# Last projection of a hybrid decoder layer: 8 of its 22 feature blocks by seven quarter products in place of eight, with the residual kept in DRAM meanwhile

## The chip, the core and the metric

The kernel runs on one core of a Trainium2 chip. The metric is the time of one execution on the device, in microseconds (us); the kernel before takes 1056.22 us (median of 3 runs, 1055.83 to 1057.02). A core has TensorE (PE; "PEld" is its weight load), VectorE (DVE), ScalarE (ACT), GpSimd (POOL) and SyncE (SP), which here only issues DMA transfers. PE writes to PSUM, 8 banks of 128 x 512 f32; all else lies in SBUF or DRAM.

## What is computed

One layer on 512 tokens of width 1024: a gated mixer of three branches, then a gated feed-forward part, then a norm. The change touches the last product of the feed-forward part:

```python
x = x + merged @ w_o[i]
x = x + conv_ffn(rmsnorm(x, ln2_g[i]), ffn_w_up[i], ffn_conv_w[i], ffn_conv_b[i], ffn_w_down[i])
...
return rmsnorm(x, final_g)

def conv_ffn(u, w_up, conv_w, conv_b, w_down):
    h = causal_dwconv(u @ w_up, conv_w, conv_b)
    a, v = h[..., :D_FF], h[..., D_FF:]
    return (jax.nn.silu(a) * v) @ w_down        # (512 x 2816) @ (2816 x 1024), f32
```

## The kernel before

Every f32 operand is split in two parts that PE takes as f32r: a high part (an ACT copy) and a low part (a DVE subtraction, operand minus high). A product is then three matmuls: high by high, high by low, low by high. `mm3` (lines 215 to 222) issues them in that order, so the low part of the weights is first wanted after two thirds of a group.

The work is a list of **jobs** (`Job`, line 72). A job is one piece of weights, at most 1 MiB, and a body that multiplies with it. While job n runs, `prepare` (lines 1281 to 1292) has queued, in this order: DVE makes the low part of job n+1 (`low`, line 204); ACT makes the high part of job n+2 in two halves (`cast`, line 184); SP fetches the weights of job n+3 (`fetch`, line 174). There are two buffers for raw weights, three for high parts and two for low parts. The order on PE, ACT, DVE and POOL is the order in which the program issues the instructions (`ORDERED`, line 1304); every engine takes its instructions in order, so one that waits holds up all behind it. SP's order is set by the scheduler of the framework.

Small work beside the matmuls stands in generators. `step()` (line 143) advances each by one piece; bodies call it between their tiles. `T()` hands out 54 SBUF tiles of 128 x 512, `MM()` and `SM()` four PSUM banks each.

The stages at the end of the program (`program`, line 1098) are:

- **wo_jobs** (line 936), the product with w_o, 8 jobs; it adds to the residual tiles X1[tb, h] (token block tb of 4, column half h), which lie in 8 of the 54 tiles from there to the end.
- **up_jobs** (line 1022), 22 jobs of 256 columns each, with 48 matmuls of 512 columns. `up_evac` (line 998) takes each tile out of PSUM (ACT line 1000, DVE line 1003 twice), applies silu (line 1005) and multiplies the two halves on POOL (line 1008). `later` (line 1010) then splits the feature block k of 22 into `ACTS[k]`, high fh (ACT line 1016) and low fl (DVE line 1017); the blocks 0 to 3 lie in `wide`.
- **down_jobs** (line 1075), the last projection. For each column half h there are 6 jobs: five of 4 feature blocks (48 matmuls: 4 token blocks x 4 blocks x 3) and one of 2 (24 matmuls). The four token blocks accumulate in four banks over all 22 blocks. For h = 0 the result is added to X1 (line 1078) and the first part of the final norm is done; for h = 1 the last two jobs are held and run token block by token block, each followed by the second part of the norm and the stores to the output.

In all the last projection has 2 x 4 x 22 x 3 = 528 matmuls of 512 columns.

Of the kernel before, what the change touches and what calls it, by code (L numbers as in the profile page):

```python
# [10 lines left out]
F32 = mybir.dt.float32  # L11
F32R = mybir.dt.float32r
# [4 lines left out]
P = 128  # L17
# [11 lines left out]
SH = 16  # L29
DFF = 2816  # L30
KF = DFF // P
C_Q, C_K, C_V = 0, AW, 2 * AW
C_POOL = 3 * AW
C_Z = C_POOL + D
# [37 lines left out]
class Job:  # L72


    def __init__(self, parts, k, c, body):
        self.parts, self.k, self.c, self.body = parts, k, c, body
        self.raw = self.split = None
        self.late = self.short = False


@with_exitstack
def trunk(ctx: ExitStack, tc, out, x, rel_bias, ln1_g, w_in, b_gate, w_a, pool_w, pool_scale, w_b,
# [23 lines left out]
    def T(name, dt=F32, shape=(P, S)):  # L106
        return big.tile(list(shape), dt, name=name, tag="t")

    def MM(name):
        return psum.tile([P, S], F32, name=name, tag="mm")  # L110
# [55 lines left out]


    def fetch(job, cuts=1):
        raw = job.raw = wraw.tile([P, job.k, job.c], F32, name="raw", tag="raw")
        at = 0  # L170
        for src in job.parts:
            n = src.shape[-1] // cuts
            for i in range(cuts):
                sp.dma_start(raw[:, :, at:at + n], src[:, :, i * n:(i + 1) * n])
                at += n

    def cast(job, cuts=1, spread=False):

        w = job.c // cuts
        job.high = whp.tile([P, job.k, job.c], F32R, name="wh", tag="wh")  # L180

        def high(i):
            o = slice(i * w, (i + 1) * w)
            act.copy(job.high[:, :, o], job.raw[:, :, o])  # L184

        def at(i):
            high(i)
            if i + 1 < cuts:
                second.append(lambda: at(i + 1))

        if spread:
            second.append(lambda: at(0))
            return
        for i in range(cuts):
            high(i)
# [16 lines left out]
    def wsrc(w, k0, k1, c0, c1):  # L212
        return w[k0 * P:k1 * P, c0:c1].rearrange("(k p) c -> p k c", p=P)

    def mm3(ps, wh, wl, xh, xl, ks, first=True, last=True, flip=False):

        n, total = 0, 3 * len(ks)
        for a, b in ((wh, xh), (wh, xl), (wl, xh)):
            for k in ks:
                l, r = (b(k), a(k)) if flip else (a(k), b(k))  # L220
                pe.matmul(ps, l, r, start=first and n == 0, stop=last and n == total - 1)  # L221
                n += 1
# [18 lines left out]
            yield Job([wsrc(w, 0, nk, c0 + i * P, c0 + i * P + width)], nk, width, body)  # L241

    def jobs_b(parts_of, c, xh, xl, nk, evac, kstep=4, mk=None, blocks=range(4), tail=0,
               turn_over=False):


        acc = {}
        starts = list(range(0, nk, kstep))
        held = []

        def use(k0, k1, ws, tb):
            wh, wl = ws
            mm3(acc[tb][:, :c], lambda k: wh[:, k - k0, :], lambda k: wl[:, k - k0, :],
                lambda k: xh(k, tb), lambda k: xl(k, tb), range(k0, k1),
                k0 == 0, k1 == nk, flip=True)

        for n, k0 in enumerate(starts):
            k1 = min(nk, k0 + kstep)

            def body(ws, n=n, k0=k0, k1=k1):  # L260
                if n == 0:
                    for tb in blocks:
                        acc[tb] = (mk or MM)("pb")
                late = n >= len(starts) - tail
                if late:
                    held.append((k0, k1, ws))
                if late and n < len(starts) - 1:
                    return
                for tb in blocks:
                    for a in (held if late else [(k0, k1, ws)]):  # L270
                        use(*a, tb)
                    if k1 == nk:
                        evac(tb, acc[tb])
                    if tb % 2:
                        step()
            job = Job(parts_of(k0, k1), k1 - k0, c, body)
            job.short = len(blocks) < 4
            if turn_over and n == len(starts) - 1:
                job.late = True

                def body(ws, job=job, inner=body):
                    late_split.append(job.prepare(later=True))
                    inner(ws)
                job.body = body
            yield job
# [643 lines left out]
    def load_x1():  # L929
        nxt["g2"] = grow(ln2_g[0])  # L930
        for tb in range(4):
            for h in range(2):
                t = X1[tb, h] = T("x1")
                sp.dma_start(t, x[tb * P:(tb + 1) * P, h * S:(h + 1) * S])

    def wo_jobs(pair, h):
        def evac(tb, ps):
            t = X1[tb, h]
            dve.tensor_tensor(t, t, ps, OP.add)
            if h == 0:  # L940
                nxt[tb] = norm_early(t, nxt["g2"])
                return
            if "uh" not in nxt:
                nxt["uh"] = upool.tile([P, KD, S], F32R, name="uh2", tag="uh")
                nxt["ul"] = upool.tile([P, KD, S], F32R, name="ul2", tag="ul")
            v0, xg0 = nxt[tb]
            us = [T("u0"), T("u1")]
            it = norm_late(t, nxt["g2"], v0, lambda xg1: ((us[0], xg0), (us[1], xg1)))
            next(it)

            def rest():
                next(it, None)
# [45 lines left out]
    def up_evac(m, ps):  # L998
        t = HC[m] = T("hc")
        act.activation(t, ps, AF.Identity, bias=ff["c1"][:, ff["b"] + m:ff["b"] + m + 1], scale=fw(2, m))  # L1000
        for k in range(2):
            sh = 2 - k
            dve.scalar_tensor_tensor(t[:, sh:], ps[:, :S - sh], fw(k, m), t[:, sh:], OP.mult, OP.add)  # L1003
        if m < KF:
            act.activation(t, t, AF.Silu)
            return
        a = HC[m - KF]
        pool.tensor_tensor(a, a, t, OP.mult)  # L1008

        def later():  # L1010
            yield
            k = m - KF
            if k == 0:
                wide.extend(ypool.tile([P, 4, S], F32R, name=n, tag="xs") for n in ("fh", "fl"))
            h, l = (t[:, k, :] for t in wide) if k < 4 else (T("fh", F32R), T("fl", F32R))
            act.copy(h, a)
            dve.tensor_sub(l, a, h.bitcast(F32))
            ACTS[k] = (h, l)

        running.append(later())  # L1020

    def up_jobs():
        held = []
# [48 lines left out]

    fin = {}

    def down_jobs(h):
        def evac(tb, ps):
            t = X1[tb, h]
            dve.tensor_tensor(t, t, ps, OP.add)
            if h == 0:
                fin[tb] = norm_early(t, fin["g"])  # L1080
                return
            v0, xg0 = fin[tb]
            for _ in norm_late(t, fin["g"], v0, lambda xg1: ((xg1, xg1), (xg0, xg0))):
                xg1 = _
            for i, o in ((1, xg1), (0, xg0)):
                sp.dma_start(out[tb * P:(tb + 1) * P, i * S:(i + 1) * S], o)

        return jobs_b(lambda k0, k1: [wsrc(w_down, k0, k1, h * S, h * S + S)], S,
                      lambda k, tb: ACTS[k][0][:, tb * P:(tb + 1) * P],
                      lambda k, tb: ACTS[k][1][:, tb * P:(tb + 1) * P], KF, evac,  # L1090
                      mk=(MM, SM)[h], tail=2 if h else 0)


    class Call:
# [3 lines left out]
    def program():  # L1098
# [26 lines left out]
        for pair in range(2):  # L1125
            for h in range(2):
                yield from wo_jobs(pair, h)
            if pair == 0:
                yield Call(ff_cols)
        yield from up_jobs()  # L1130
        yield Call(lambda: fin.setdefault("g", grow(final_g)))
        yield Call(finish)
        yield from down_jobs(0)
        yield from down_jobs(1)

    jobs = list(program())
    weights = [j for j in jobs if isinstance(j, Job)]
# [200 lines left out]
```

## Time and profile before

| | |
|---|---|
| median of 3 runs | 1056.22 us |
| the execution that was profiled | 1058.24 us |
| its span, first to last instruction | 1056.4 us |
| PE busy | 1044.1 us (99% of the span) |
| DVE, ACT, POOL busy | 576.7, 430.9, 134.9 us |
| read from DRAM | 110.87 MB |
| stage of line 221, tile pu (up_jobs), in the chain | 229.33 us, x1056 |
| stage of line 221, tile pb after it (down_jobs), in the chain | 119.69 us, x528 |
| from the last matmul to the end | 7.3 us |

In the views a group of instructions reads: line, engine, operation, result <- operands by tile name, shapes, number (x); then busy us and mean ns of one; then the idle time of the engine before them and what ended it. "wh" and "wl" are the high and low part of weights, "raw" the weights as fetched, "pb" the PSUM tile of the last projection. A view by windows gives the busy time of each engine in each stretch of the span, then the granted clock of PE (PEclk, 1.00 is full), the busy share of the 16 DMA engines, and the GB/s that they moved.

### The profile page before, as it was taken

Reading aid. Unit: us, or ns where it says so; the run is one execution under the profiler, and the core shown is the slowest. Engines: PE = TensorE matmul, PEld = TensorE weight load, DVE = VectorE, ACT = ScalarE, POOL = GpSimd, SP = SyncE. Lnnn points to the kernel's source line nnn. Section 1 sums busy time; section 2 is a strip of 40 time slices with the busy share of each in tenths; the row PEclk is TensorE's granted clock in tenths of the full one; section 3 lists DMA queues with packets and bytes.
Section 4 is the critical chain, followed back from the end, with each engine's and each line's share of the span. In section 5 each row is a group of like instructions: output and inputs, shape, how many; then the busy total and the mean of one; then the engine's idle time right before and its main releaser. Section 6 shows DMA issues by size and latency. Waiting matters only on the chain.

```text
span 1056.4 us, 13018 instructions
## 1 busy us (share of the span) xinstructions
PE 1044.1 (99%) x5268; PEld 872.5 (83%) x5268; DVE 576.7 (55%) x777; ACT 430.9 (41%) x698; POOL 134.9 (13%) x118
## 2 busy tenths in 40 slices
PE   8999999999999999999999999999999999999997
PEld 8878889898788887787888888898888888888885
DVE  5552523245667538576658756766556565532315
ACT  6343412232545633567555323554444434431311
POOL 1580000000000001100143500002111111110100
PEclk9999999999999999999999999999999999999999
DMA  7236233242221355542252426542322323232312
GB/s 241 77 116 180 80 102 94 86 124 67 83 80 60 81 152 137 150 126 57 69 150 83 157 80 217 184 141 80 117 83 94 105 81 120 80 120 77 103 60 80
DMA packets 116426, 115.50 MB, mean 109 GB/s; under 512 B 5235, under 2 KB 101302, under 8 KB 116367
## 3 DMA queue, kind: packets, MB, share of 16 engines
q1 hardware_dynamic: 116367, 114.68, 35.9%
q8 instruction: 41, 0.67, 0.3%
q14 instruction: 18, 0.15, 0.0%
HBM read 110.87 MB, written 2.22 MB: 107 GB/s over the span
## 4 chain that ended last, share of the span: by engine, by line
PE 91%; DMA 2%; issue 2%; ACT 1%; DVE 1%; SPq 1%; POOL 0%; DVEq 0%; ACTq 0%; POOLq 0%
PE pa L221 35%; PE pu L221 22%; PE pb L221 19%; PE pqk L221 7%; DMA al<-ad 1%; PE ps L512 1%; PE pu L1036 1%; PE ppw L221 1%; PE po L551 1%; PE pt L539 1%; DVE wl L204 1%; DMA raw<-in_w_in_dram 1%; SPq L468 1%; PE py L808 1%; PE pyo L814 1%
## 5 line engine op out<-in xcount | busy, mean ns | idle before, releaser
L204 DVE TENSOR_TENSOR wl<-raw,wh 128x2048 fp32r<-128x2048 f32 (+3 forms) x94 | 219.2, 2333 | 137.9 <-PE pb L221 67.6
L184 ACT CAST wh<-raw 128x1024 fp32r<-128x1024 f32 (+2 forms) x186 | 187.2, 1025 | 104.4 <-PE pb L221 41.0
L221 PE MATMUL pa<-uh,wh 128*128 128x512 f32 x384 | 99.3, 400 | 0.3 <-ACT wh L184 0.3
L1003 DVE SCALAR_TENSOR_TENSOR hc<-pu,fcol,hc 128x510 f32<-128x510 f32 x88 | 65.9, 749 | 54.5 <-ACT hc L1000 52.8
L221 PE MATMUL pa<-ul,wh 128*128 128x512 f32 x384 | 95.0, 389 | 0.0
L221 PE MATMUL pa<-uh,wl 128*128 128x512 f32 x384 | 94.9, 389 | 0.0
L221 PEld LDWEIGHTS pa<-ul,wh 128*128 128x128 f32 x384 | 72.1, 188 | 15.3
L221 PEld LDWEIGHTS pa<-uh,wl 128*128 128x128 f32 x384 | 72.1, 188 | 14.9
L221 PE MATMUL pu<-uh,wh 128*128 128x512 f32 (+1 forms) x352 | 83.7, 380 | 0.0
L221 PEld LDWEIGHTS pa<-uh,wh 128*128 128x128 f32 x384 | 69.9, 188 | 16.5 <-issue 1.7
L221 PE MATMUL pu<-ul,wh 128*128 128x512 f32 (+1 forms) x352 | 83.5, 379 | 0.0
L221 PE MATMUL pu<-uh,wl 128*128 128x512 f32 (+1 forms) x352 | 83.5, 379 | 0.0
L221 PEld LDWEIGHTS pu<-ul,wh 128*128 128x128 f32 x352 | 64.2, 188 | 12.5
L221 PEld LDWEIGHTS pu<-uh,wl 128*128 128x128 f32 x352 | 64.2, 188 | 12.4
L221 PEld LDWEIGHTS pu<-uh,wh 128*128 128x128 f32 x352 | 64.1, 188 | 12.5
L1000 ACT ACTIVATE hc<-pu,fcol,fcol 128x512 f32<-128x512 f32 x40 | 31.2, 780 | 82.1 <-PE pu L221 82.1
L1008 POOL TENSOR_TENSOR hc<-hc 128x512 f32<-128x512 f32 x22 | 31.5, 1433 | 223.3 <-DVE hc L1003 188.2
L787 POOL TENSOR_TENSOR xd<-xc,dec 128x512 f32<-128x512 f32 x6 | 6.4, 1063 | 362.9 <-DVE xc L778 344.3
L533 ACT ACTIVATE sb<-sb,nm 128x128 f32<-128x128 f32 (+1 forms) x72 | 30.1, 419 | 47.0 <-DVE nm L530 33.3
L221 PE MATMUL pb<-wh,fl 128*128 128x512 f32 x176 | 47.7, 389 | 0.0
L221 PE MATMUL pb<-wl,fh 128*128 128x512 f32 x176 | 47.7, 389 | 0.0
L221 PE MATMUL pb<-wh,fh 128*128 128x512 f32 x176 | 47.7, 389 | 0.0
(273 smaller groups left out, 1597.6 us busy)
## 6 DMA issues: line engine op xcount, KB each, us to landing
raw<-in_w_in_dram SPq DMA_DIRECT2D x25, 1024.0 KB
raw<-in_ffn_w_up_dram SPq DMA_DIRECT2D x22, 1024.0 KB
raw<-in_w_in_dram SPq DMA_DIRECT2D x20, 512.0 KB
raw<-in_ffn_w_down_dram SPq DMA_DIRECT2D x10, 1024.0 KB
raw<-in_w_o_dram SPq DMA_DIRECT2D x8, 1024.0 KB
raw<-in_w_in_dram SPq DMA_DIRECT2D x6, 768.0 KB
raw<-in_w_b_dram SPq DMA_DIRECT2D x4, 1024.0 KB
al<-ad SPq DMA_DIRECT2D x16, 256.0 KB
```

What stands on the lines that cost most here:

```text
L184: act.copy(job.high[:, :, o], job.raw[:, :, o])
L204: (eng or dve).tensor_tensor(l[:, :, o], job.raw[:, :, o], h[:, :, o].bitcast(F32), OP.subtract)
L221: pe.matmul(ps, l, r, start=first and n == 0, stop=last and n == total - 1)
L468: sp.dma_start(V[g, n][32 * tb:32 * tb + 32, :384], t[n:P:4, :384])
L512: pe.matmul(pss[i][:, o:o + w * P], q[r, n * P:(n + 1) * P], k[r, kb * P:(kb + w) * P], start=True, stop=True)
L533: act.activation(sb[:, off:off + w * P], sb[:, off:off + w * P], AF.Exp, bias=nm[:, n, h:h + 1], accum_out=ls[:, n, h:h + 1])
L539: pe.transpose(pt[:, o:o + P], sb[:, o:o + P], eye)
L551: pe.matmul(po[DH * hh:DH * hh + DH, n * P:(n + 1) * P], V[g, kb + i][:, (2 * c + hh) * DH:(2 * c + hh + 1) * DH], probs[2 * c + hh, nb][: ...
L808: pe.matmul(py[DH * i:DH * i + DH, j * P:(j + 1) * P], xc[:, o:o + DH], als[j // 2][:, lo:lo + P], start=True, stop=True)
L1000: act.activation(t, ps, AF.Identity, bias=ff["c1"][:, ff["b"] + m:ff["b"] + m + 1], scale=fw(2, m))
L1003: dve.scalar_tensor_tensor(t[:, sh:], ps[:, :S - sh], fw(k, m), t[:, sh:], OP.mult, OP.add)
L1008: pool.tensor_tensor(a, a, t, OP.mult)
```

## The change

The feature blocks 0 to 7 (KS = 8) leave the ordinary jobs, which now take the blocks 8 to 21 (14 in each half: three jobs of 4 blocks and one of 2). For the 8 blocks, the tokens are cut in two halves of 256, the features in even and odd blocks, and the columns in two halves of 512. These are three two-way cuts, so the product is one of 2 x 2 quarters by 2 x 2 quarters: 8 products of quarters, done here as 7, with sums and differences of quarters as operands and results. Each product has 2 token blocks x 4 feature blocks x 3 = 24 matmuls of 512 columns, with 1 MiB of weights.

- In up_jobs, `later` splits an odd block k < 8 as before, and of an even one only the first 256 tokens (f0). `sums_of` makes the sums for each of the four pairs of blocks: 4 DVE instructions on 128 x 256, 2 ACT copies and 2 DVE subtractions on 128 x 512.
- The weights of two quarters (second column half) are loaded to the buffer "uh" that up_jobs has read until its end (`load_w`). Differences of quarters are made by DVE on 128 x 2048 (`diff`), four in all; one lies in p1's body, three in the `cast` of the jobs five, seven and four (`form`), ahead of the high part. The jobs five, seven and six fetch nothing.
- X1 is written to DRAM after the fourth job of up_jobs (`put_x1`; the scheduler puts these 8 transfers of 256 KiB into SP's order from wo_jobs on, each behind the last addition to its tile), and read back into the buffer "ul" at the end of up_jobs (`get_x1`).
- The order of the jobs: p2, plain, p1, p5, plain, p7, plain, p6, plain (2 blocks), p4, p3; then the four plain jobs of the second column half. p2 and p4 accumulate into the banks of the plain jobs of the first half, p3 into those of the second. p1, p5, p6 and p7 go to the SM banks and are taken out by ACT copies and DVE additions.
- The first part of the final norm moves from the evacuation into a generator (`early`), one step later.

```diff
 def fetch(job, cuts=1):
+        if job.load:
+            job.load()
+            return
...
 def cast(job, cuts=1, spread=False):
         w = job.c // cuts
+        if job.form:
+            job.raw = job.form()
         job.high = whp.tile([P, job.k, job.c], F32R, name="wh", tag="wh")
...
+    def put_x1():
+        nxt["x1"] = dram.tile([4, 2, P, S], F32, name="x1d")
+        for tb, h in X1:
+            sp.dma_start(nxt["x1"][tb, h], X1[tb, h])
+    def get_x1():
+        back = upool.tile([P, KD, S], F32, name="x1b", tag="ul")
+        for h in range(2):
+            for tb in range(4):
+                X1[tb, h] = back[:, 2 * tb + h, :]
+                sp.dma_start(X1[tb, h], nxt["x1"][tb, h])
...
+            if k >= KS or k % 2:
+                h, l = T("fh", F32R), T("fl", F32R)
+                act.copy(h, a)
+                dve.tensor_sub(l, a, h.bitcast(F32))
+                ACTS[k] = (h, l)
+                if k < KS:
+                    yield
+                    for _ in sums_of(k // 2, HC[k - 1], a):
+                        yield
+                return
             if k == 0:
-                wide.extend(ypool.tile([P, 4, S], F32R, name=n, tag="xs") for n in ("fh", "fl"))
-            h, l = (t[:, k, :] for t in wide) if k < 4 else (T("fh", F32R), T("fl", F32R))
-            act.copy(h, a)
-            dve.tensor_sub(l, a, h.bitcast(F32))
-            ACTS[k] = (h, l)
+                wide.extend(ypool.tile([P, 4, S], F32R, name=n, tag="xs") for n in ("sh", "sl"))
+            t = T("f0", F32R)
+            act.copy(t[:, :256], a[:, :256])
+            dve.tensor_sub(t[:, 256:], a[:, :256], t[:, :256].bitcast(F32))
+            FS[0, k // 2] = (t[:, :256], t[:, 256:])
         running.append(later())
+    FS = {}
+    def sums_of(p, f0, f1):
+        lo, hi = slice(0, 256), slice(256, S)
+        sa, sb = T("sa"), T("sb")
+        dve.tensor_tensor(sa[:, lo], f0[:, hi], f1[:, hi], OP.add)
+        dve.tensor_tensor(sa[:, hi], sa[:, lo], f0[:, lo], OP.subtract)
+        dve.tensor_tensor(sb[:, lo], f0[:, lo], f0[:, hi], OP.subtract)
+        dve.tensor_tensor(sb[:, hi], f1[:, lo], sa[:, hi], OP.subtract)
+        yield
+        ah, al = (t[:, p, :] for t in wide)
+        bh, bl = T("sbh", F32R), T("sbl", F32R)
+        act.copy(ah, sa)
+        act.copy(bh, sb)
+        yield
+        dve.tensor_sub(al, sa, ah.bitcast(F32))
+        dve.tensor_sub(bl, sb, bh.bitcast(F32))
+        FS[1, p], FS[2, p] = (ah[:, lo], al[:, lo]), (ah[:, hi], al[:, hi])
+        FS[3, p], FS[4, p] = (bh[:, lo], bl[:, lo]), (bh[:, hi], bl[:, hi])
...
+    def down():
+        n2 = KS // 2
+        quarter = lambda two, h: w_down[:KS * P, h * S:(h + 1) * S].rearrange(
+            "(k two p) c -> two p k c", two=2, p=P)[two]
+        W, acc, rs, r3 = {}, {0: {}, 1: {}}, {}, {}
+        def load_w():
+            both = upool.tile([P, KD, S], F32, name="w3", tag="uh")
+            for at in range(2):
+                W[at] = both[:, 4 * at:4 * at + 4, :]
+                sp.dma_start(W[at], quarter(at, 1))
+            get_x1()
+        def diff(out, a, b):
+            dve.tensor_tensor(out, a, b, OP.subtract)
+            return out
+        def product(ps, ws, parts, first, last):
+            wh, wl = ws
+            mm3(ps, lambda k: wh[:, k, :], lambda k: wl[:, k, :], lambda k: parts[k][0],
+                lambda k: parts[k][1], range(n2), first, last, flip=True)
+        def first_half(i):
+            return [[t[:, i * P:(i + 1) * P] for t in FS[0, p]] for p in range(n2)]
+        def second_half(tb):
+            return [[t[:, tb * P:(tb + 1) * P] for t in ACTS[2 * p + 1]] for p in range(n2)]
+        def sums(j, i):
+            return [[t[:, i * P:(i + 1) * P] for t in FS[j, p]] for p in range(n2)]
+        def add(tb, h, what):
+            dve.tensor_tensor(X1[tb, h], X1[tb, h], what, OP.add)
+        def job(parts, use, form=None, ld=None):
+            def body(ws):
+                for i in range(2):
+                    use(i, ws)
+                    step()
+            j = Job(parts, n2, S, body)
+            j.form, j.load = form, ld
+            return j
+        def p2(i, ws):
+            acc[0][i] = MM("pb")
+            product(acc[0][i], ws, second_half(i), True, False)
+        def p1(i, ws):
+            ps = SM("p1")
+            product(ps, ws, first_half(i), True, True)
+            add(i, 0, ps)
+            rs[i] = T("r1")
+            act.copy(rs[i], ps)
+            if i:
+                diff(W[0], W[1], W[0])
+        def p5(i, ws):
+            ps = SM("p5")
+            product(ps, ws, sums(1, i), True, True)
+            add(i, 1, ps)
+            add(2 + i, 1, ps)
+        def p7(i, ws):
+            ps = SM("p7")
+            product(ps, ws, sums(3, i), True, True)
+            r3[i] = T("r3")
+            act.copy(r3[i], ps)
+        def p6(i, ws):
+            ps = SM("p6")
+            product(ps, ws, sums(2, i), True, True)
+            dve.tensor_tensor(rs[i], rs[i], ps, OP.add)
+            dve.tensor_tensor(r3[i], r3[i], rs[i], OP.add)
+            def rest():
+                yield
+                add(2 + i, 0, r3[i])
+                yield
+                add(i, 1, rs[i])
+                yield
+                add(2 + i, 1, r3[i])
+            running.append(rest())
+        def p4(i, ws):
+            product(acc[0][2 + i], ws, second_half(2 + i), False, True)
+            add(2 + i, 0, acc[0][2 + i])
+            running.append(early(2 + i))
+        def p3(i, ws):
+            acc[1][i] = SM("pb")
+            product(acc[1][i], ws, sums(4, i), True, False)
+        one = job([quarter(0, 0)], p1)
+        five = job([], p5, lambda: diff(one.raw, W[0], one.raw), lambda: None)
+        def formed():
+            diff(W[1], W[1], one.raw)
+            return W[0]
+        seven = job([], p7, formed, lambda: None)
+        six = job([], p6, lambda: W[1], lambda: None)
+        four = job([quarter(1, 0)], p4, lambda: diff(four.raw, four.raw, W[1]))
+        plain = blocks_of(0, acc[0], (0, 1), (2, 3))
+        yield Call(load_w)
+        yield job([quarter(1, 0)], p2)
+        yield next(plain)
+        yield one
+        yield five
+        yield next(plain)
+        yield seven
+        yield next(plain)
+        yield six
+        yield from plain
+        yield four
+        yield job([quarter(1, 1)], p3)
+        yield from blocks_of(1, acc[1], (0, 1), ())
...
+    def early(tb):
+        yield
+        fin[tb] = norm_early(X1[tb, 0], fin["g"])
+    def blocks_of(h, acc, opened, keep):
         def evac(tb, ps):
             t = X1[tb, h]
             dve.tensor_tensor(t, t, ps, OP.add)
             if h == 0:
-                fin[tb] = norm_early(t, fin["g"])
+                running.append(early(tb))
...
-        return jobs_b(lambda k0, k1: [wsrc(w_down, k0, k1, h * S, h * S + S)], S,
-                      lambda k, tb: ACTS[k][0][:, tb * P:(tb + 1) * P],
-                      lambda k, tb: ACTS[k][1][:, tb * P:(tb + 1) * P], KF, evac,
-                      mk=(MM, SM)[h], tail=2 if h else 0)
+        return jobs_b(lambda k0, k1: [wsrc(w_down, KS + k0, KS + k1, h * S, h * S + S)], S,
+                      lambda k, tb: ACTS[KS + k][0][:, tb * P:(tb + 1) * P],
+                      lambda k, tb: ACTS[KS + k][1][:, tb * P:(tb + 1) * P], KF - KS, evac,
+                      mk=(MM, SM)[h], tail=2 if h else 0, acc=acc, opened=opened, keep=keep)
...
-        yield from up_jobs()
+        for i, job in enumerate(up_jobs()):
+            yield job
+            if i == 3:
+                yield Call(put_x1)
         yield Call(lambda: fin.setdefault("g", grow(final_g)))
         yield Call(finish)
-        yield from down_jobs(0)
-        yield from down_jobs(1)
+        yield from down()
```

In `jobs_b` the banks of `opened` token blocks are taken over (no new start), and those in `keep` are neither closed nor evacuated. `mm3`, `low`, the buffers of weights and the tail of the last two jobs are unchanged.

More of the change, by code (lines that the diff above doesn't have):

```diff
@@ L31 @@
 KF = DFF // P
+KS = 8
 C_Q, C_K, C_V = 0, AW, 2 * AW
@@ L78, in __init__ @@
         self.late = self.short = False
+        self.load = self.form = None
 @with_exitstack
@@ L243, in jobs_b @@
     def jobs_b(parts_of, c, xh, xl, nk, evac, kstep=4, mk=None, blocks=range(4), tail=0,
-               turn_over=False):
-        acc = {}
+               turn_over=False, acc=None, opened=(), keep=()):
+        acc = {} if acc is None else acc
         starts = list(range(0, nk, kstep))
@@ L254, in use @@
                 lambda k: xh(k, tb), lambda k: xl(k, tb), range(k0, k1),
-                k0 == 0, k1 == nk, flip=True)
+                k0 == 0 and tb not in opened, k1 == nk and tb not in keep, flip=True)
         for n, k0 in enumerate(starts):
@@ L262, in body @@
                     for tb in blocks:
-                        acc[tb] = (mk or MM)("pb")
+                        if tb not in opened:
+                            acc[tb] = (mk or MM)("pb")
                 late = n >= len(starts) - tail
@@ L271, in body @@
                         use(*a, tb)
-                    if k1 == nk:
+                    if k1 == nk and tb not in keep:
                         evac(tb, acc[tb])
@@ L1073, in trunk @@
     fin = {}
-    def down_jobs(h):
+    def early(tb):
+        yield
+        fin[tb] = norm_early(X1[tb, 0], fin["g"])
+    def blocks_of(h, acc, opened, keep):
         def evac(tb, ps):
```

## The prediction

> **What bounds the kernel now.** First the page: busy times, and the shares of the chain of work that ended last.
>
> ```profile
> PE 1044.1 (99%) x5268; PEld 872.5 (83%) x5268; DVE 576.7 (55%) x777; ACT 430.9 (41%) x698; POOL 134.9 (13%) x118
> ...
> PE 91%; DMA 2%; issue 2%; ACT 1%; DVE 1%; SPq 1%; POOL 0%; DVEq 0%; ACTq 0%; POOLq 0%
> ```
> PE is busy 99% of the span and holds 91% of the chain, so a matmul removed where nothing else is late is time removed. Whether PE is the bound in this stage is read from the chain in order of time (start, length, what):
>
> ```profile
> 700.04 229.33 PE pu L221 x1056
> 929.37 119.69 PE pb L221 x528
> 1049.09 0.70 DVE x L1078
> ```
> From 700 us to 1049.1 us the chain never leaves PE. The last projection is 528 matmuls in one piece. They begin at 929.21 in the timeline and end at 1049.09, where the last addition starts: 119.88 us, 0.227 us each. After it only 7.3 us of norm and stores remain, which the change does not touch. Then what the other engines have left, from the groups of that stage, each shape apart:
>
> ```profile
> L204 DVE TENSOR_TENSOR wl<-raw,wh 128x2048 fp32r<-128x2048 f32 x9 | 20.6, 2292 | 52.8 <-PE pb L221 48.8 <-issue 3.2 <-ACT wh L184 0.8
> L184 ACT CAST wh<-raw 128x1024 fp32r<-128x1024 f32 x17 | 17.0, 1047 | 35.1 <-PE pb L221 23.3 <-DMA raw<-in_ffn_w_down_dram 11.8
> L1078 DVE TENSOR_TENSOR x<-x,pb 128x512 f32<-128x512 f32 x8 | 5.5, 682 | 3.0 <-PE pb L221 3.0
> ...
> L204 DVE TENSOR_TENSOR wl<-raw,wh 128x1024 fp32r<-128x1024 f32 x2 | 2.4, 1224 | 17.2 <-PE pb L221 17.2
> ```
> The columns after the bar are busy us, mean ns of one, and idle time before. A low part of a 1 MiB job costs DVE 2.29 us, a high part ACT 2 x 1.05, an addition out of PSUM 0.68. The windows, later, show DVE busy 38 of 119.7 us. There is room on average. But the new jobs of 24 matmuls last 24 x 0.227 = 5.44 us where one of 48 lasts 10.88, so each handover is looked at alone. The timeline at the start of the stage:
>
> ```profile
> 929.21 1.07 PE L221 MATMUL pb<-wh,fh 128*128 128x512 f32 x4
> ...
> 934.21 0.69 DVE L1017 TENSOR_TENSOR fl<-hc,fh 128x512 fp32r<-128x512 f32 x1 [1.83 <-ACT fh L1016]
> ...
> 934.65 1.07 PE L221 MATMUL pb<-wh,fh 128*128 128x512 f32 x4
> 934.82 2.29 DVE L204 TENSOR_TENSOR wl<-raw,wh 128x2048 fp32r<-128x2048 f32 x1
> ...
> 936.46 1.07 PE L221 MATMUL pb<-wl,fh 128*128 128x512 f32 x4
> ...
> 942.38 2.00 ACT L184 CAST wh<-raw 128x1024 fp32r<-128x1024 f32 x2 [6.30 <-DMA raw<-in_ffn_w_down_dram]
> ```
> The first matmul is at 929.21. DVE finishes the last two fl of up_jobs (line 1017) before it makes the low part of the second job, from 934.82 to 937.11. Of 24 matmuls, PE is through at 934.65.
>
> **What goes.** Eight products of quarters become seven: 24 matmuls x 0.227 = **-5.44 us**. The ordinary jobs keep their 2 x 4 x 14 x 3 = 336, the seven products have 168, together 504.
>
> **What comes in, on PE's path.** I place the new jobs at PE's pace and put each DVE and ACT instruction behind the one ahead of it on its engine, with the durations above; differences of 128x2048 count as 2.29, the price of the same operation on line 204. PE wants the low part 8 matmuls (1.81 us) after a job begins, 4 in a job of two blocks.
>
> - p2 runs 929.21 to 934.65. The plain job behind it wants its low part at 936.46; DVE has it at 937.11, as above, since the fl still stand ahead. PE waits **+0.65 us**. Before, the first job was twice as long, and this did not show.
> - The plain job ends at 946.2. p1's low part is ready at 939.4. DVE makes five's difference by 941.7, ACT its high part by 943.8; its low part waits for a buffer until 946.2 and ends at 948.5, wanted at 953.4.
> - p1 ends at 951.6. Behind its two additions DVE makes a difference (954.7) and the low part of the second plain job (957.0, wanted at 958.9: **1.9 us to spare**). Then the difference of the job seven, four additions for p5, and seven's low part, 964.4, wanted at 969.8.
> - The rest in the same way, ready and wanted: third plain job 970.3 and 975.2, p6 977.4 and 986.1, the short plain job 985.5 and 990.6, p4 994.1 and 997.0, **p3 1000.9 and 1002.4, the first job of the second half 1006.2 and 1007.9**. The last two are narrow because DVE has six additions and two small instructions of the norm ahead of p3's low part.
> - PSUM: p1, p5, p7 and p6 take the four SM banks in turn. Each bank is emptied a whole plain job before it is wanted again. Nothing on the path.
>
> **The transfers.** The buffers uh and ul come free when up_jobs' last matmuls have read them, at about 927.5 (ul) and 929.3 (uh). SP then issues two tiles of X1, the two quarters and six more tiles, 4.2 MB, and the second plain job's weights queue behind, 5.2 MB in all. One fetch of 1 MiB alone takes 5.2 us (issued 937.17, and ACT goes on at 942.38, last line above). For many at once, the windows:
>
> ```profile
> 640.00:645.00 5.00, 5.00 (x23) 4.14 (x23) 3.23 (x4) 2.77 (x4) 0.00 (x0) 1.00 1.04 388
> ...
> 929.40:1049.10 119.70, 119.65 (x528) 98.76 (x527) 37.95 (x48) 27.70 (x42) 6.77 (x5) 1.00 0.24 80
> 1049.10:1056.40 7.30, 0.00 (x0) 0.00 (x0) 3.07 (x8) 0.93 (x3) 0.00 (x0) 0.66 0.39 144
> ```
> In 5 us with the eight loads of x and a fetch together, 388 GB/s were moved. At that rate the first quarter lands at about 935 (wanted by DVE at 939.4) and the plain job's weights at 944 (wanted by ACT at 950.3). Cost: nothing, hidden by p2 and the first plain job. If the cover were gone, each us of lateness over 4.5 and over 8 would be a us on PE.
>
> **The writes of X1** stand in SP's order ahead of fetches, each behind an addition that DVE has made before the low part that the next fetch waits for anyway, so they add 0.37 us of issue (a DMA issue of line 174) and 0.65 us of transfer each at 388 GB/s, in a stage where fetches leave pauses. One place has no slack, the opening of up_jobs, on ACT:
>
> ```profile
> 697.43 2.00 ACT L184 CAST wh<-raw 128x1024 fp32r<-128x1024 f32 x2 [5.34 <-DMA raw<-in_ffn_w_up_dram]
> 699.33 1.06 ACT L322 CAST uh<-uT 128x512 fp32r<-128x512 f32 x2
> ```
> ACT waits 5.34 us for weights, and the uh that PE multiplies at 699.96 is copied only behind them. The last write, 256 KiB issued at about 688.1, is nearly through when these weights are issued at 691.25. Between 0 and its 0.65 us; I take **+0.2 us**.
>
> **The sums in up_jobs.** A subtraction on 512 columns takes 0.69, on 1024 1.22, on 2048 2.29 us, so 1.04 us per 1000 columns and 0.16 fixed, 0.42 for 256. Per pair of blocks DVE gets 4 x 0.42 + 2 x 0.73 and is spared 0.30, some 2.8 us, and ACT 0.9, while PE works 21.8 us on the two jobs of the pair. By the windows DVE is busy 135.6 of 229.4 us in this stage, and with four PSUM banks 16 us lie between a tile's end and its bank's next use. At one end this costs nothing, at the other, were DVE full there, 4 x 2.8 = 11 us; it can gain nothing, as it only adds work. At 59% I take 0, and the other end goes to the slow side of the rivals.
>
> **Sum.** -5.44 + 0.65 + 0.2 = -4.6 us. Made against the profiled execution: span 1056.4 to 1051.8, and with the 1.84 us around it 1058.24 to 1053.6. The median of the runs shown is 2.0 us below that execution, so **1051.6 us**. Measurement of this kernel can tell about 0.2% (2.1 us) from no change.
>
> **The rivals.**
>
> - *The handovers give the gain back* (0.20). The three spares of 1.5 to 1.9 us, and five's chain of difference, high and low part, rest on durations of one stage. POOL's multiplications stretch a low part from 2.29 to 3.38 us (timeline, 910.53, beside POOL line 1008), and semaphores cost some 0.05 us a step. One us lost at each of three: 1054.6; half of this case is still faster by 0.2%, half is not. For it: DVE has about 20 us of work in the first 28 us of the stage (seven operations of 2.29, four of about 0.75, two additions). Against it: POOL works 6.8 us in the whole stage.
> - *The burst of transfers is late: slower* (0.08). At the kernel's mean of 109 GB/s the 5.2 MB take 48 us, the second plain job's weights land at 977, and PE waits some 25 us less the 4.6: about 1077 us. Below 238 GB/s it begins to cost, below about 195 GB/s the gain is gone. For it: windows over a whole stage show 80 GB/s; against it: that is what was asked, and 388 when more was.
> - *A wait lets PE's clock fall* (0.03). In the last window, with no matmul, the granted clock is 0.66 over 7.3 us: full for about 2.3 us, then half. A wait of 4 us for the first quarter, with as long at half clock behind it as it took to fall, gives 1051.6 + 4 + 1.2 = 1056.8. [...] The trace agrees that the clock falls; no run here shows how it returns.
> - *No wait at all* (0.05): a full 5.44, 1050.8 us.
> - *The change doesn't do what it says* (0.02): were products still eight, the time would be 1057 us.
>
> My forecast (0.62) is 1050.8 to 1052.6. The range 1050.4 to 1055.2 leaves out the far part of the handovers' case, the burst, the clock and the eight products, under 2 in 10. Faster by over 0.2% (below 1054.1): 0.62 + 0.05 + half of 0.20 = 0.77; within: 0.10 + 0.03 + 0.02 = 0.15; slower: 0.08.
>
> **What would show it.** 504 matmuls in the last projection in some 115 us, about 0.7 us of PE idle before the third group of the first plain job, ended by DVE's low part; DVE busy some 64 us in the stage (38, and four differences 9.2, three low parts more 6.9, fourteen additions more 9.7); no ACT or DVE wait on a quarter or on X1; a DMA window near 390 GB/s from 929 to 942; and up_jobs beginning within 0.7 us of 700. It is wrong if PE shows gaps at the start of the second plain job, p3 or the second half's first job, if DVE waits on the quarters, or if the granted clock leaves 1.00 before 1044.

## The result: 1052.08 us, from 1056.3

The changed kernel takes 1052.08 us (median of 5 runs, 1051.29 to 1052.42); the kernel before took 1056.3 us in the runs beside it. The ratio is 0.9954 (95% interval 0.994 to 0.9969): faster by 3.3 to 6.3 us. The forecast was 1051.6 us, range 1050.4 to 1055.2. The execution that was profiled took 1051.72 us, its span is 1049.5 us.

The page of the changed kernel, busy times and shares of the chain:

```profile
PE 1038.3 (99%) x5244; PEld 867.5 (83%) x5244; DVE 613.5 (58%) x824; ACT 442.4 (42%) x716; POOL 137.8 (13%) x118
...
PE 94%; issue 2%; ACT 1%; DVE 1%; DMA 1%; POOL 0%; SPq 0%; DVEq 0%; ACTq 0%; POOLq 0%
```
24 matmuls fewer, 5.8 us less of PE, 36.8 us more of DVE; PE is the bound as before. The chain in order of time (start, length, what) says where the 36.8 us went, which is beside PE:

```profile
698.40 229.15 PE pu L228 x1056
927.55 5.45 PE pb L228 x24
933.04 2.25 DVE wl L211
935.34 9.36 PE pb L228 x40
...
988.22 54.41 PE pb L228 x240
1042.65 0.70 DVE x1b L1257
```
The last projection lasts from 927.55 to 1042.65, 115.10 us where it was 119.72. In these 115 us the chain leaves PE once, for 2.3 us, to a low part of weights on DVE (line 211, which was 204). The windows of this stage and of a part of the burst of transfers (length; busy PE, PEld, DVE, ACT, POOL; PEclk; DMA share; GB/s):

```profile
927.55:1042.65 115.10, 114.53 (x505) 94.17 (x503) 65.27 (x70) 35.84 (x52) 9.57 (x5) 1.00 0.34 119
932.00:937.00 5.00, 4.47 (x20) 3.40 (x19) 4.61 (x3) 2.26 (x3) 0.00 (x0) 1.00 1.05 396
```
DVE is busy 65.27 us of the stage, the clock stays at 1.00, and the burst moves 396 GB/s.

**The spans cannot simply be subtracted.** They differ by 6.9 us: 4.62 in the last projection, 0.18 in the stage of up_jobs, 0.46 behind the last matmul, and 1.64 before wo_jobs begins (639.04 against 640.68), where the change does nothing; PE waits there 1.5 us for a copy of ACT in the execution of before, 0.4 in that of after, and 0.4 in experiment 2 too, which is the old kernel up to there. Experiment 4, the changed kernel up to there, begins wo_jobs at 640.59, so this part is the spread of executions. The 0.46 is no gain either: what lies outside the span is 2.22 us in after (1051.72 less 1049.5) and 1.84 in before, so that 0.38 of it comes back. The table therefore goes by stages: from the start of wo_jobs to the 1056 matmuls of up_jobs in one piece ("opening"), this piece, and the last projection.

| kernel | time, us (median) | ratio to before (95%) | opening | up_jobs | last projection |
|---|---|---|---|---|---|
| before | 1056.3 to 1056.6 | | 59.36 | 229.33 | 119.72 |
| **after** | 1052.08 | 0.9954 (0.994 to 0.9969) | 59.36 | 229.15 | **115.10** |
| 1 fl later | 1051.56 | 0.9954 (0.9941 to 0.9968) | 59.37 | 229.24 | 114.27 |
| 2 journey of X1 alone | 1057.41 | 1.0009 (1.0 to 1.0018) | 59.37 | 229.41 | 119.71 |
| 3 burst + 2 MiB | 1053.84 (one run) | | 60.23 | 229.41 | 115.11 |
| 4 burst + 6 MiB | 1061.74 | 1.0054 (1.004 to 1.0068) | 59.37 | 229.15 | 125.69 |
| 5 DVE work ahead of p3 | 1055.84 (one run) | | 59.37 | 229.15 | 118.85 |
| 6 p7 twice | 1057.67 | 1.001 (1.0001 to 1.0019) | 60.13 | 229.42 | 120.55 |
| 7 as 1, writes by ACT | 1051.16 | 0.9947 (0.9933 to 0.996) | 59.37 | 229.15 | 114.27 |
| 8 as 2, writes by ACT | 1056.49 | 0.9999 (0.999 to 1.0007) | 59.37 | 229.15 | 119.72 |
| 9 burst + 4.5 MiB | 1058.02 (one run) | | 59.37 | 229.40 | 121.34 |
| 10 fewer plain jobs between | 1053.88 (one run) | | 59.48 | 229.42 | 116.81 |

The one wait, in the timeline of the changed kernel:

```profile
932.39 0.69 DVE L1037 TENSOR_TENSOR fl<-hc,fh 128x512 fp32r<-128x512 f32 x1 [1.83 <-ACT fh L1036]
933.00 4.49 DVE L211 TENSOR_TENSOR wl<-raw,wh 128x2048 fp32r<-128x2048 f32 x2
...
933.74 1.07 PE L228 MATMUL pb<-wh,fl 128*128 128x512 f32 x4
935.34 1.20 PE L228 MATMUL pb<-wl,fh 128*128 128x512 f32 x4 [0.53 <-DVE wl L211]
```
DVE waits 1.83 us for ACT, makes the last fl of up_jobs, and only then the low part. A group of four matmuls follows the one before it after 0.907 us; this one begins 1.60 us after the group before, 0.69 late, and takes 1.20 us in place of 1.07.

### The profile page after: what moved, and what is told of

Its sections match the earlier page's. It is cut to its first block, busy times and chain, and to the rows that moved or that the text cites. A ratio compares the mean times of both kernels' runs of the same rounds, so it can differ in the third digit from the quotient of the medians.

```text
span 1049.5 us, 13068 instructions
## 1 busy us (share of the span) xinstructions
PE 1038.3 (99%) x5244; PEld 867.5 (83%) x5244; DVE 613.5 (58%) x824; ACT 442.4 (42%) x716; POOL 137.8 (13%) x118
## 3 DMA queue, kind: packets, MB, share of 16 engines
HBM read 115.07 MB, written 4.32 MB: 114 GB/s over the span
## 4 chain that ended last, share of the span: by engine, by line
PE 94%; issue 2%; ACT 1%; DVE 1%; DMA 1%; POOL 0%; SPq 0%; DVEq 0%; ACTq 0%; POOLq 0%
PE pa L228 35%; PE pu L228 22%; PE pb L228 17%; PE pqk L228 9%; PE p L228 2%; PE ps L521 1%; PE pu L1211 1%; PE ppw L228 1%; PE po L560 1%; PE pt L548 1%; PE py L817 1%; PE pyo L823 1%; DMA raw<-in_w_in_dram 1%; PE pst L834 0%; ACT wh L191 0%
## 5 line engine op out<-in xcount | busy, mean ns | idle before, releaser
L191 ACT CAST wh<-raw 128x1024 fp32r<-128x1024 f32 (+3 forms) x188 | 189.4, 1025 | 86.9 <-PE pa L228 32.9
L919 DVE TENSOR_TENSOR sg<-sg,pa 128x512 f32<-128x512 f32 x24 | 16.1, 685 | 41.9 <-PE pa L228 41.8
L228 PE MATMUL pqk<-uh,wh 128*128 128x512 f32 x144 | 36.7, 397 | 0.0
L228 PE MATMUL pqk<-ul,wh 128*128 128x512 f32 x144 | 35.6, 389 | 0.0
```

The costliest lines, as they stand in the source:

```text
L919: dve.tensor_tensor(s, s, ps, OP.mult)
```

## The experiments

My theory was that of the forecast: the last projection is PE's 504 matmuls and this one wait; the journey of X1, the transfers, the sums and the other handovers lie beside them. The rivals: the transfers or the journey cost something that chance hides, and the handovers are nearly late.

**1. The fl later.** `finish` ends all pending small work ahead of the last projection. Without it the last fl are made in p2's body, at its first step.

```diff
-        yield Call(finish)
         yield from down()
```

> One line less than in the changed kernel: the pending small work of up_jobs is no longer finished ahead of the last projection, so DVE makes the low part of the first plain job before the second of the two last fl. Theory (the gain is 24 matmuls less one wait of 0.7 us for that low part): DVE has it at about 933 to 934, wanted at 934.65; the wait goes, no new one comes, the last projection takes 114.4 us in place of 115.2, and the time is about 4.9 to 5.4 us below before, 0.7 below the changed kernel. Rival (the low part is late for another reason, the buffer or the high part): the 0.5 to 0.7 us stay. Rival (the fl or the high part of p1, now later, are late themselves): the wait moves to p1 or to the short plain job, 0 to 1 us.

Measured: 114.27 us and no wait of PE in the stage, so the wait and what follows it cost 0.83 us. That is 504 x 0.2267, so PE is never late in this stage. DVE's order, and POOL beside it, in the timeline:

```profile
929.68 1.59 POOL L1029 TENSOR_TENSOR hc<-hc 128x512 f32<-128x512 f32 x1 [4.09 <-DVE hc L1024]
...
930.04 3.38 DVE L211 TENSOR_TENSOR wl<-raw,wh 128x2048 fp32r<-128x2048 f32 x1
933.35 0.68 DVE L1037 TENSOR_TENSOR fl<-hc,fh 128x512 fp32r<-128x512 f32 x1
```
The low part now stands ahead of the last fl. It is stretched from 2.29 to 3.38 us beside POOL, which is busy for the first 1.23 of them, and is still early.

**2 and 8. The journey of X1 alone**, in the kernel before, its writes issued by SP (2) as in the change, or by ACT (8):

```diff
+        nxt["x1"] = dram.tile([4, 2, P, S], F32, name="x1d")
+            sp.dma_start(nxt["x1"][tb, h], X1[tb, h])      # 8: act.dma_start
...
-        yield from up_jobs()
+        for i, job in enumerate(up_jobs()):
+            yield job
+            if i == 3:
+                yield Call(put_x1)
...
         yield Call(finish)
+        yield Call(get_x1)
         yield from down_jobs(0)
```

> The kernel before with the journey of the residual alone: X1 is written to DRAM and read back as in the changed kernel, all 22 feature blocks stay in ordinary jobs. Theory (transfers hidden): the last projection keeps 119.9 us and 528 matmuls, the opening of up_jobs is late by 0 to 0.65 us, the time is within 0.2% of before. Rival (the journey itself costs or brings something, so that the gain of the change is not that of the matmuls alone): 1 us or more either way.

> The kernel before with the journey of the residual alone, its writes issued by ACT at the fifth job of up_jobs. Theory: the 0.9 us that the journey alone cost in the median came from the opening of up_jobs, so the time is that of before, within 0.3 us. Rival (it is the reading back, or chance): 0.5 to 1.0 us more than before again.

Measured: by SP 0.95 us more than before by the medians (ratio 1.0009, 1.0 to 1.0018), by ACT 0.1 us less (0.9999, 0.999 to 1.0007). The last projection is 119.71 and 119.72 us: reading X1 back costs nothing. What the writes by SP cost is not in the stages of experiment 2's profiled execution, where the opening is 59.37 us; at 1056.44 us that execution is the second shortest of eleven. A wait that may be the cost shows in two others (3 and 6, see there). The intervals of 2 and 8 overlap, so that the writes by ACT are cheaper is likely, not shown.

**3, 4 and 9. A larger burst.** 8, 24 or 18 extra writes of 256 KiB on SP's queue, behind the reads of X1 and ahead of the second plain job's weights. They are read by nobody.

```diff
             get_x1()
+            more = dram.tile([24, P, S], F32, name="more")   # 3: 8, 9: 18
+            for i in range(24):
+                sp.dma_start(more[i], ACTS[KF - 1][1].bitcast(F32))
```

> As the 6.3 MB burst, with 8 extra writes of 256 KiB (2.1 MB). The weights of the second plain job are issued some 6 us later than in the changed kernel, at about 941.5 on its clock, and land at about 949, where ACT wants them at 948.7 and PE has 2 us more. Theory (a cover of 8 us): no wait at the second plain job, the last projection 115.1 us as in the changed kernel. Rival (the transfers had little to spare): 3 to 6 us more.

> The changed kernel with 24 more writes of 256 KiB to DRAM (6.3 MB) queued behind the transfers at the start of the last projection and ahead of the weights of the second plain job; what is written is not used. Theory (those weights had 8 us to spare, and each us beyond is a us of PE): they land 16 to 18 us later, PE waits about 6 us (4 to 8) at the start of the second plain job, and the gain over before is gone: 1 to 3 us slower than before. Rival (the cover is deeper than the forecast had it, a job further): 0 to 2 us over the changed kernel. Rival (transfers that come together slow each other, or SP's queue itself blocks): 10 us or more.

Measured: 115.11 us with 2 MiB, so these transfers had at least that much room; 125.69 us with 6 MiB, 10.6 more than after. (The profiled execution is the longest of four; by the medians of the whole times it is 9.7.) The timeline of experiment 4:

```profile
956.07 1.07 PE L228 MATMUL p<-wl,sh 128*128 128x512 f32 x4
...
962.12 1.04 ACT L191 CAST wh<-raw 128x1024 fp32r<-128x1024 f32 x1 [11.79 <-DMA raw<-in_ffn_w_down_dram]
964.65 2.08 PE L228 MATMUL pb<-wh,fh 128*128 128x512 f32 x4 [7.51 <-ACT wh L191]
966.52 1.91 PE L228 MATMUL pb<-wh,fl 128*128 128x512 f32 x4
```
The weights come late, ACT waits 11.79 us and PE 7.51; that is the rival of the late burst, produced on purpose. PE resumes 7.67 us late, and the rest of the 10.6 us, 2.9, is in the pace behind: groups of 1.07 us take 1.91. The granted clock (sixth number behind the length) falls and returns in these two windows of 1 us:

```profile
960.00:961.00 1.00, 0.00 (x0) 0.00 (x0) 0.00 (x0) 0.00 (x0) 0.00 (x0) 0.69 0.17 68
...
970.00:971.00 1.00, 1.00 (x5) 0.82 (x4) 1.00 (x3) 0.00 (x0) 0.00 (x0) 0.69 1.05 410
```
Between them it is 0.50. Full clock for a part of a window and half for the rest gives 0.69 if it falls at 960.38 and returns at 970.62, 10.24 us later. The wait is in my range of 4 to 8 us, and the weights are issued 17.7 us later than in after (954.65 here, 935.35 there, the stage 1.56 later here); so the 10.6 is not my rival of slower transfers, though it has its size. The whole time is 5.3 us above before where I expected 1 to 3, and what I had not counted is the clock; experiment 9 takes a shorter wait to see what that costs.

> The changed kernel with 18 extra writes of 256 KB (4.5 MiB, of a finished tile, read by nobody) on SP's queue, ahead of the weights of the second plain job. With 24 such writes PE waited 7.5 us for these weights and the stage grew by 10.6 us, 2.9 us more than the wait; with 8 it did not wait at all. 1 MiB took about 2.6 us there, so 6 writes fewer bring the weights 3.9 to 4.5 us sooner: a PE wait of 3.0 to 3.6 us. My theory: a wait of such a length costs itself plus one window of 3.4 us at half clock, 1.7 us: the last projection 115.1 + 3.3 + 1.7 = 120 us (119 to 121). Rival: only a wait of 7 us and more lowers the clock at this place (another place, where 1.9 us were enough, had a second wait beside it): the wait alone, 118 to 118.7 us, with a granted clock of 1.00 in every microsecond behind it.

Measured: 121.34 us, the wait 3.50 us as expected. The windows of 1 us of experiment 9 give the clock:

```profile
957.00:958.00 1.00, 0.00 (x0) 0.00 (x0) 0.00 (x0) 1.00 (x2) 0.00 (x0) 0.88 0.00 0
958.00:959.00 1.00, 0.00 (x0) 0.00 (x0) 0.00 (x0) 1.00 (x2) 0.00 (x0) 0.50 0.00 0
...
964.00:965.00 1.00, 1.00 (x4) 0.74 (x4) 1.00 (x3) 0.00 (x0) 0.00 (x0) 0.71 1.03 401
```
It is 0.50 in all windows between. 0.88 and 0.71 place the fall at 957.76 and the return at 964.58, 6.82 us later. PE, idle from 955.7, resumes at 959.24 and so works 5.34 us at half clock, half of which, 2.67, is lost. With the 3.66 us by which it resumes late that is 6.33; the stage grew by 6.24. The rival (no fall) is out. My 119 to 121 us was too low: the half clock lasted 6.82 us, not the 3.4 that I had counted from experiment 5.

**5. DVE work ahead of p3**, the narrowest handover: two additions of 128 x 512 more, twice, into tiles that nobody reads.

```diff
             def rest():
                 yield
+                for _ in range(2):
+                    dve.tensor_tensor(T("more"), r3[i], rs[i], OP.add)
                 add(2 + i, 0, r3[i])
```

> The changed kernel with four more DVE additions on 128 x 512 (their result is not used), two of them in the piece ahead of p4's low part and two ahead of p3's. In the trace of the changed kernel p3's low part was ready 0.5 us before PE wanted it (the forecast had 1.5), with DVE's additions stretched from 0.69 to 1.1 us where POOL multiplies beside them. Theory (that handover is the narrowest): DVE is later by 2.8 to 4.4 us there, and PE waits 2.3 to 3.9 us at p3 and nowhere else; the last projection takes 117.4 to 119.0 us. Rival (there is slack that the reading missed): under 1 us.

Measured: 118.85 us, 3.75 more than after. The timeline of PE in experiment 5:

```profile
1000.39 1.07 PE L228 MATMUL pb<-wh,sbl 128*128 128x512 f32 x4
1003.24 1.68 PE L228 MATMUL pb<-wl,sbh 128*128 128x512 f32 x4 [1.78 <-DVE wl L211]
1004.72 1.91 PE L228 MATMUL pb<-wh,sbh 128*128 128x512 f32 x4
```
PE resumes 1.94 us late. The clock falls and returns in these windows, and is 0.50 between them:

```profile
1003.00:1004.00 1.00, 0.76 (x3) 0.62 (x4) 1.00 (x3) 0.18 (x1) 0.13 (x1) 0.87 0.00 0
...
1007.00:1008.00 1.00, 1.00 (x6) 0.82 (x5) 0.68 (x1) 0.00 (x0) 1.00 (x1) 0.92 0.54 209
```
It is halved from 1003.74 to 1007.16, 3.42 us, which loses 1.7. So the 118.85 us lies in my range of 117.4 to 119.0 by luck: the wait was below the 2.3 to 3.9 that I expected, and the clock, which I had not counted, made up the rest. The spare ahead of p3 in the changed kernel was thus real but small, as its own timeline shows:

```profile
993.21 3.00 POOL L339 TENSOR_TENSOR xg<-x1b,grow 128x512 f32<-128x512 f32 x2 [61.51 <-issue]
...
993.59 4.38 DVE L1111 TENSOR_TENSOR x1b<-x1b,r 128x512 f32<-128x512 f32 x4
998.01 2.27 DVE L211 TENSOR_TENSOR wl<-raw,wh 128x2048 fp32r<-128x2048 f32 x1
...
1000.75 1.07 PE L228 MATMUL pb<-wl,sbh 128*128 128x512 f32 x4
```
The low part is ready at 1000.28 and wanted at 1000.75: 0.47 us. Four additions take 4.38 us beside POOL's multiplications; four others in this stage, beside no POOL, take 2.47.

**6. p7 twice**, into the same bank, the first product overwritten: 24 matmuls given back, nothing else.

```diff
             product(ps, ws, sums(3, i), True, True)
+            product(ps, ws, sums(3, i), True, True)
             r3[i] = T("r3")
```

> The changed kernel with the 24 matmuls of p7 issued twice in place (the second time starts the bank anew, so the result is the same). Theory (PE at 0.227 us a matmul is all that the product costs): 5.44 us more than the changed kernel, which puts it at 0.7 to 1.0 us from before, with the last projection at 120.6 us. Rival (part of a product's price lies in DVE and ACT beside it): less than 4.5 us, since more of PE covers them.

Measured: the last projection 120.55 us, 5.45 more than after, and 1057.67 us in all. The removed product is worth its 24 x 0.227 us. This execution is also later at the opening of up_jobs, 60.13 in the table of stages. It is plainest in experiment 3; the waits of PE there, and then ACT's timeline:

```profile
PE pu L228 <- ACT uh L331: 0.9, 1, 0.9
```

```profile
697.70 2.00 ACT L191 CAST wh<-raw 128x1024 fp32r<-128x1024 f32 x2 [6.28 <-DMA raw<-in_ffn_w_up_dram]
```
ACT waits 6.28 us for weights (4.97 in after), and the uh that PE wants is copied behind them, from 699.60 on. The lateness comes in all sizes, and it goes with ACT's wait for these weights. "Opening" and "up_jobs" of the table, added:

| execution | ACT waits for these weights, us | opening + up_jobs, us |
|---|---|---|
| after, 4, 5, 7, 8 | 4.32 to 5.05 | 288.51 or 288.52 |
| 1 | 5.26 | 288.61 |
| before | 5.34 | 288.69 |
| 2, 9, 10 | 5.41 to 5.54 | 288.77 to 288.90 |
| 6 | 5.66, and 0.23 a job earlier | 289.55 |
| 3 | 6.28 | 289.64 |

Before has no writes and is 0.18 us late here; after has the writes by SP and is not late. That the writes make these weights late is thus not shown; the two largest sizes, though, are in executions with writes by SP.

**7. The fl later, and the writes by ACT**, to join what 1 and 8 gave.

> The version with the fl later, and the 8 writes of X1 issued by ACT at the fifth job of up_jobs, where the program has them, in place of SP from wo_jobs on. Theory (the writes cost something only in the opening of up_jobs, in some executions, where the journey alone showed 0.9 us more in the median): the opening keeps 13.5 us in every execution, the issues on ACT (8 x 0.4 us) are hidden in up_jobs, the last projection is 114.3 us, and the time is 0.5 to 1.0 us below the version with the fl later. Rival (the writes cost nothing anywhere): the same time as that version, within 0.3 us. Rival (ACT's issues hold up the taking out of PSUM): up_jobs longer than 229.4 us.

Measured: 1051.16 us (1050.8 to 1051.44), ratio 0.9947 (0.9933 to 0.996), the fastest of all here. Its last projection is 0.83 us shorter than that of the change. It is 0.4 us below version 1, less than the 0.5 to 1.0 that I expected, and the whole times of 1, 7 and the change are not told apart by their intervals. The opening (59.37) and up_jobs (229.15) are as expected.

**10. Fewer plain jobs between the products.** The second and third plain job are done behind p6, ahead of the short one (the expectation names one plain job too many there).

```diff
         yield job([quarter(1, 0)], p2)
-        yield next(plain)
         yield one
         yield five
         yield next(plain)
         yield seven
-        yield next(plain)
         yield six
```

> The changed kernel with the second and the third plain job of two feature blocks taken out from between the products and done behind them: p2, p1, p5, plain, p7, p6, plain, plain, plain, the two-block job, p4, p3. The work is the same. What it tells: whether the order (ordinary jobs, which last 10.9 us of PE, between products, which last 5.4) is what hides DVE's and ACT's preparation. My theory: p1 and p5 then follow a product directly; a product's preparation (differences, two casts, a low part) takes 5 to 6.5 us of DVE and ACT against 5.4 us of PE, so PE waits 0.5 to 0.9 us at each of p1, p5 and the plain job behind them: the last projection 116 to 118 us instead of 115.1, no wait long enough to lower the clock. Rival A: the preparation is early enough through the buffers' depth and nothing is lost: 114.9 to 115.3. Rival B: the waits add up behind one another until one passes 1.9 us and the clock falls: above 119.

Measured: 116.81 us, 1.7 more than after. Here the waits of PE in the last projection are three:

```profile
PE p L228 <- DVE wl L211: 0.7, 2, 0.5
PE p L228 <- ACT wh L191: 0.4, 1, 0.4
```
p1 waits for its low part, p5 for its high and its low part, and PE resumes 0.7, 0.6 and 0.4 us late; a further gap of 0.3 us lies in the plain job behind. I had expected 0.5 to 0.9 at each of the three jobs. The clock is 1.00 in every window of 1 us from 930 to 960. So the order hides work: with fewer plain jobs between, 1.7 of the 4.6 us are gone.

## Why the prediction was right, step by step

- **-5.44 for the removed product**: shown, from both sides. Experiment 1 is 5.45 us below before in this stage, experiment 6 gives 5.45 back.
- **+0.65 for the low part behind the last fl**: the mechanism is shown (one wait, at the third group of the first plain job, gone when the fl come later). The size is 0.83: PE resumes 0.69 late, which is the 0.65, and its next group takes 0.13 longer, which I had not counted.
- **+0.2 at the opening of up_jobs**: not a constant cost. The place is as narrow as the forecast said, but it varies from execution to execution, from 0 to 1.1 us over after, and before itself loses 0.18 there, so the profiled execution of after gains 0.18 where the forecast lost 0.2. By the medians of experiment 2 the writes by SP cost 0.95 (0 to 1.9); with ACT as the writer -0.1 (-1.1 to 0.7). That the opening is where the 0.95 goes is argued, not shown: the execution profiled there has 0.09 more than before.
- **The burst costs nothing**: shown, 2 MiB more cost nothing in this stage, 6 MiB cost 10.6 us. The 388 GB/s taken from before stand beside 396 here. DVE's first difference starts right behind a low part and no quarter is waited for.
- **Sums in up_jobs, 0**: shown. The piece is 229.15 us in after, and 229.15 to 229.42 in the experiments with the sums and without them (8 has none, and 229.15); what differs goes with the opening, as the table in 6 shows.
- **The spares**: 1.9 us for the second plain job's low part became 1.97 (ready 955.26, wanted 957.23), 1.7 for the second half's first job 1.4, but 1.5 for p3 only 0.47. This was the weakest term. I counted POOL's 6.8 us (9.57 in after) as too little to matter; it falls just where DVE has six additions, and makes 4.38 us of 2.47 for four of them. The forecast held since the spare was larger than the loss, by 0.47 us; what counts is where POOL's work falls, not its sum.
- **The sum.** From wo_jobs to the last matmul, after's execution shows -4.80 against -4.6; by the medians the time fell by 4.2. In the opening and the last projection alone it is -4.62, where 0.18 more for the wait and 0.2 less for the opening cancel. That is luck, and small beside the 5.44.
- **The rival of the clock** was 4 us of wait and 1.2 behind it. No run shows the 1.2; it was my estimate, from a half clock that lasts as long as the clock took to fall. No wait of this kind is in the change, but three were made: behind lateness of 1.94, 3.66 and 7.67 us came a loss of 1.8, 2.6 and 2.9, so 1.2 was less than half the price at 3.66 us. Half clock lasted 3.42, 6.82 and 10.24 us in the experiments 5, 9 and 4, about two and three times the shortest; what sets these lengths is not shown.

Not tried: X1 left in SBUF throughout, which would take the journey away (its 8 tiles beside the 48 that the splits and sums hold are more than the 54 there are).

## What to carry to other kernels

A matmul taken away on a full PE is worth its time only if each handover keeps its spare: place jobs at PE's pace, and check the moment when DVE, ACT and the transfer are through against the moment when PE wants them. Put short jobs, whose preparation lasts as long as they do, between long ones: experiment 10, with two fewer of them between, lost 1.7 us. A handover that was late by 1.94 us cost 3.75, since the clock was at half for 3.42 us behind it (a gap of 1.9 us seems also to have left the clock alone, see below), while one that was late by 0.69 us cost 0.83.

## What the runs showed of the chip that I had not expected

- **The clock.** Behind 1.78 us of PE idle in experiment 5 the clock was halved, and it fell after PE had resumed (1003.24, fall at 1003.74). Gaps of 0.5 us in after, of 0.4 and 0.5, some 4 us apart, in experiment 10, and of 0.96 and 1.50 in before (ended at 410.85 and 12.92) left it at 1.00. One of 1.9 us in experiment 4 (PE, tile pcb, waits for DVE line 825) seems to have done so too. That is an estimate from the mean clock of this execution, 0.994 over a span of 1061.6 us, or 11.7 to 13.8 us at half: beside the 10.24 above, a further 3.42 would leave at most 0.1 for the 6.8 us behind the last matmul, where after has 4.8 of 6.9 at half. So the length of a gap seems not to decide alone, and what does stays open. Full clock came back 3.92, 5.34 and 5.97 us after PE had resumed in the experiments 5, 9 and 4; what brings it back is not shown.
- **DVE beside POOL.** A low part of 128 x 2048 takes 2.29 us alone and 3.38 where POOL multiplies during its first 1.23 us (experiment 1): 1.09 us, nearly all of that time, is lost to DVE. Four additions lose 1.91 of the 2.62 us in which POOL runs beside them (ahead of p3: 4.38 us, against 2.47 alone). Why is not shown.
